# The second output projection of a hybrid decoder as seven block products instead of eight

## The chip, the core and the metric

The kernel runs on one core of a Trainium2 chip. The metric is the device time of one execution in microseconds (us), less is better. The engines that the text names: TensorE (PE, with its weight loads as PEld), VectorE (DVE), ScalarE (ACT), GpSimd (POOL) and SyncE (SP), which issues nearly all DMAs.

## The reference

One step of a two-layer decoder: a prompt of 2048 positions and a sample group of 8 x 4 positions, model width 1024, branch width 2048. Layer 0 is gated linear attention, layer 1 sliding-window attention. What the change touches is the end of layer 1: the attention output `o`, gated, times the second output weight (2048 x 1024), added to the residual stream.

```python
def swa_out(o, gate, w_out):
    bsz, seq_len = o.shape[:2]
    return (o.reshape(bsz, seq_len, BRANCH_WIDTH) * jax.nn.silu(gate)) @ w_out
...
q_p, g_p = swa_query(hp, b_norm[j], b_w_in[j], b_q_norm[j], pos_p)
hp = hp + swa_out(swa_banded(q_p, k_p, v_p, b_sinks[j]), g_p, b_w_out[j])
```

## The kernel before

**Numbers as pairs.** Every large product is fp32 in effect: each operand is held as two fp16 tiles, high and low, and a block product is three passes (`PASSES`: high x high, high x low, low x high). `split` makes such a pair: the high part on ACT, the low part on DVE or POOL. A product of a 128 x 128 block (stationary) with a 128 x 512 block (moving) is three matmuls.

**Stages.** (1) Layer 0: heads 0 to 3, each in four blocks of 512 positions (`Blk`), with the sample group beside it. (2) The first output projection, 16 chunks of 128 positions (`a_out`), with residual, norm and the transposed input of layer 1 (`uT`). (3) Attention of layer 1: 4 groups x 16 chunks = 64 blocks (`BBlk`), in a loop over n = 0..66 in which iteration n projects block n and does the scores of block n-2 and the values of block n-3. `ORDER` is a hand-written interleaving of the two attention parts with the projection steps ("f"), and while `pin` is set, TensorE keeps the order in which the program emits its matmuls. In n = 64..66 there is no block left to project, and the steps "f" are the first chunks of the last stage. (4) The second output projection.

**Last stage.** `out_steps(wo, half, ogs, finish, c)` takes one chunk c and one half of the 1024 output columns: it loads four transposed tiles of the gated output from DRAM (`ogd2`, written by `spill_og`), runs 16 contraction tiles x 3 passes = 48 matmuls into one bank of tag `pj` (two buffers), and `b_finish` adds the residual (`hd`) on DVE and stores. All 16 chunks for half 0 come first, then all 16 for half 1, so each chunk is loaded and transposed twice. `out_sample` does the same for the 32 sample positions, with the weight as the stationary operand.

**Weights ahead of time.** `GroupW` (weights of layer 1) and `wob` (the second output weight, two halves) are prepared beside the earlier stages: `Unit.prepare` loads 256 KB into `wraw` (three buffers), splits it into `pst` (two buffers), and stores the pair to DRAM from POOL's queue. These steps stand in a list `prep`, from which the blocks of layer 0 take `PR[j]` at a time and the first output projection five per chunk; `behind` gives them a lower priority. Later `steps()` fetches them as tiles `W` (12 buffers of 512 KB): eight for the next group at chunk 12 of each group, eight for half 0 at chunk 12 of the last group, eight for half 1 inside the last stage.

Outside the pinned loop a scheduler with its own model of the engines decides the order of instructions on each engine; engines then run their queues strictly in that order. A tile with a tag shares that tag's buffers; a buffer comes free when the last reader of the tile before is done.

Of the kernel before, what the change touches and what calls it, by code (L numbers as in the profile page):

```python
# [9 lines left out]
F32 = mybir.dt.float32  # L10
# [34 lines left out]
OSC = 1.0 / (SOG * SW)  # L45
OA = SQ * SST
# [8 lines left out]
PR = (1, 4, 2, 0)  # L55
# [17 lines left out]
def _body(tc, nc, cp, sb, ps, dr, i, o):  # L73
# [69 lines left out]
    ogd2 = [dr.tile([P, 2, BW], F16, tag=f"oge{c}", name=f"oge{c}") for c in range(NCH)]  # L143
# [478 lines left out]
    def sproj_steps(tiles, nk, act_hi_lo):  # L622

        box = []

        def one(x, w):
# [207 lines left out]
    wob = [out_w(i["b_w_out"][0], half, None) for half in range(2)]  # L834
    prep = [f for w in gw + wob for f in w.prepare()]
# [169 lines left out]
    def out_steps(wo, half, ogs, finish, c):  # L1005
        ot = []

        def load():
            t = T("uT", [P, 4, 8, P], F16, 4)
            for q in range(4):  # L1010
                ot.append(t[:, q])
                nc.sync.dma_start(ot[q], ogs[c][:, q % 2, q // 2 * D : q // 2 * D + D], transpose=True)

        st, box = proj_steps(lambda: PT("pj", [P, 512], bufs=2), lambda k, a: ot[k // 8 * 2 + a][:, k % 8, :], wo, 16)
        return [load] + st + [lambda: finish(half, c, box[0])]

# [34 lines left out]
    def out_sample(wo, half, finish_s):  # L1051
        st, total = sproj_steps(wo.cols(4), 16, lambda: ogTs[0])

        def fin():
            t = T("ssg", [P, 4, SMP], F32, 1)
            total(t, 0, 4, OSC)
# [21 lines left out]
    lead = 4  # L1078
    aout[0][0]()
    todo = []  # L1080
    for c in range(lead):
        todo += [aout[c + 1][0]] + aout[c][1][0] + aout[c][1][1]
    weave(prev_tail, todo)
    for c in range(lead, tail):
        aout[c + 1][0]()
        weave(aout[c][1][0] + aout[c][1][1], some(5))
        if c == 7:
            for half, w in enumerate((wo, wo1)):
                run(out_sample(w, half, a_finish_s))
# [21 lines left out]
    class BBlk:  # L1111
# [98 lines left out]
        def attend_steps(self):  # L1210
# [73 lines left out]
    class SampleB:  # L1284
# [22 lines left out]
        def steps(self):  # L1307
# [141 lines left out]
            def att_3(tq):  # L1449
# [13 lines left out]
                dve.scalar_tensor_tensor(of, pO.rearrange("p x b t -> p x (b t)"), 2.0**-20, self.sg[:, :, tk], ALU.mult, ALU.mult)  # L1463
# [17 lines left out]
    def b_finish(half, c, pp):  # L1481
        cs = slice(half * 512, half * 512 + 512)
        hr = T("E", [P, 512], F32, 2)
        nc.sync.dma_start(hr, hd[c][:, cs])
        y = T("st", [P, 512], F32, 2)
        dve.scalar_tensor_tensor(y, pp, OSC, hr, ALU.mult, ALU.add)  # L1486
        nc.sync.dma_start(o["y"][0, c * P : (c + 1) * P, cs], y)
# [12 lines left out]
    bout = [out_steps(wob[0], 0, ogd2, b_finish, c) for c in range(3)]  # L1500
    for t in range(-3, NKV * NCH):
# [11 lines left out]
        elif n < NKV * NCH + 3:  # L1513
            fill = bout[n - NKV * NCH][1:]
# [24 lines left out]
    run(out_steps(wob[0], 0, ogd2, b_finish, 3))  # L1539
# [96 lines left out]
```

## Time and profile before

| | us |
|---|---|
| median of 3 runs | 2900.65 |
| lowest, highest | 2900.28, 2902.48 |
| the profiled execution | 2899.76 |
| its span | 2898.0 |

The span runs from the first to the last instruction; 1.8 us of the profiled execution lie outside it. The stages by the span's clock: layer 0 to about 1130 us, the first output projection to about 1525, attention to about 2589, the second output projection to the end. The page gives busy times by engine, the span in 40 slices, and groups of instructions; the answers of the trace give the same for any window, and for every idle stretch of an engine what ended it.

### The profile page before, as it was taken

What the parts mean: (1) busy time and instruction counts of PE and PEld (TensorE: products, weight loads), DVE (VectorE), ACT (ScalarE), POOL (GpSimd) and SP (SyncE); (2) the same over time, 40 slices, a digit from 0 to 9 for tenths busy, and PEclk for the clock granted to TensorE, in tenths of its full rate; (3) what the DMA queues carried; (4) which work ended last, traced back from release to release, by engine and by line L of the source; (5) the groups of instructions that cost most, each with busy time, mean ns of one, the idle gap of its engine ahead of it and who ended that gap; (6) DMA issues with size and microseconds to landing.
All of it is one profiled execution on the core that took longest, in us unless ns stands there. A gap on an engine that the chain in (4) does not pass through costs nothing.

```text
span 2898.0 us, 51309 instructions
## 1 busy us (share of the span) xinstructions
PE 2769.2 (96%) x19198; PEld 1401.8 (48%) x19198; DVE 1661.5 (57%) x3543; ACT 1386.7 (48%) x3289; POOL 1012.0 (35%) x1407
## 2 busy tenths in 40 slices
PE   6899999999999999997999999999899999999999
PEld 4445444444454444444444555555555555544444
DVE  5766787687768775333214666677777767730000
ACT  6655655465556554333213555566666666620000
POOL 1241233222322221022105676566566557510000
PEclk9999999999999999998999999999999999999999
DMA  8351344124313524799866565767866777898874
GB/s 211 85 124 44 88 120 128 37 84 151 97 41 101 162 69 114 158 238 260 186 167 142 109 131 122 192 119 129 170 114 130 169 132 138 162 214 170 182 148 96
DMA packets 813331, 393.86 MB, mean 136 GB/s; under 512 B 687760, under 2 KB 740952, under 8 KB 813048
## 3 DMA queue, kind: packets, MB, share of 16 engines
q1 hardware_dynamic: 802040, 361.14, 56.3%
q0 software_dynamic: 8960, 29.37, 2.8%
q8 instruction: 150, 2.46, 0.4%
q14 instruction: 101, 0.83, 0.1%
q10 hardware_dynamic: 2080, 0.07, 0.0%
HBM read 132.61 MB, written 101.25 MB: 81 GB/s over the span
## 4 chain that ended last, share of the span: by engine, by line
PE 59%; DVE 10%; ACT 9%; DMA 9%; issue 7%; POOL 5%; SPq 1%; POOLq 0%; ACTq 0%; DVEq 0%
PE pj L99 45%; PE tr L99 6%; PE o L99 4%; PE kv L99 3%; DMA pre<-pst 2%; ACT o L1237 2%; DMA wraw<-in_a_w_in_dram 2%; DVE v L195 1%; DMA pst<-v 1%; ACT v L194 1%; PE lev L99 1%; DVE o L1232 1%; POOL pre L245 1%; DVE W L195 1%; DVE lev L1232 1%
## 5 line engine op out<-in xcount | busy, mean ns | idle before, releaser
L99 PE MATMUL pj<-W,uT 128*128 128x512 f16 x6600 | 1529.0, 381 | 6.6 <-DVE sg L475 3.4
L99 PEld LDWEIGHTS <-uT 128*128 128x128 f16 x8224 | 788.1, 98 | 892.6 <-issue 49.3
L99 PE MATMUL tr<-W,uT 128*128 128x512 f16 x1536 | 365.5, 379 | 0.0
L183 POOL TENSOR_SCALAR rs_m<-ss 128x1 f32<-128x1 f32 (+3 forms) x190 | 44.6, 235 | 757.7 <-ACT og L608 243.6
L1237 ACT ACTIVATE o<-o,mx 128x256 f32<-128x256 f32 (+1 forms) x384 | 168.6, 439 | 181.5 <-DVE mx L1232 172.1
L192 POOL TENSOR_TENSOR ogT<-og,ogT 128x512 f16<-128x512 f32 x132 | 162.1, 1228 | 168.3 <-ACT ogT L191 163.8
L99 PEld LDWEIGHTS <-X 128*128 128x128 f16 x2496 | 159.9, 98 | 120.9 <-issue 20.7
L99 PE MATMUL pj<-uT,W 128*128 128x512 f16 (+1 forms) x912 | 187.0, 356 | 27.1 <-DMA uT<-ogT 23.6
L1232 DVE CUSTOM_DVE_ANT_0 o<-o,madd,nsink 128x256 f32<-128x256 f32 (+1 forms) x384 | 184.0, 479 | 46.8 <-PE o L99 41.8
L195 DVE SCALAR_TENSOR_TENSOR v<-o,v 128x512 f16<-128x512 f32 (+1 forms) x192 | 129.0, 672 | 116.3 <-ACT v L194 98.4
L184 POOL TENSOR_TENSOR rs_r<-rs_m,mhalf 128x1 f32<-128x1 f32 (+2 forms) x186 | 185.5, 998 | 14.7
L99 PEld LDWEIGHTS <-W 128*128 128x128 f16 x2576 | 132.8, 99 | 115.0 <-issue 20.1
L1486 DVE SCALAR_TENSOR_TENSOR st<-pj,E 128x512 f32<-128x512 f32 x32 | 22.1, 692 | 269.8 <-PE pj L99 260.0
L505 POOL TENSOR_TENSOR E<-bt 128x256 f32<-128x256 f32 x96 | 74.3, 774 | 197.4 <-DVE X L192 117.7
L245 POOL DMA_DIRECT2D pre<-pst x104 | 72.3, 695 | 190.7 <-DVE pst L195 155.9
L99 PE MATMUL pj<-W,v 128*128 128x512 f16 x576 | 128.3, 379 | 0.0
L99 PE MATMUL o<-gl,X 128*128 128x256 f16 (+1 forms) x768 | 114.0, 272 | 10.2 <-DMA X<-qe 5.4
L99 PEld LDWEIGHTS <-sth 128*128 128x128 f16 x1984 | 100.3, 98 | 39.4 <-DMA sth<-v 11.2
L99 PEld LDWEIGHTS <-v 128*128 128x128 f16 x768 | 74.5, 98 | 92.6 <-issue 4.5
L646 ACT ACTIVATE ssg<-pj 128x64 f32<-128x64 f32 (+1 forms) x16 | 3.5, 240 | 236.8 <-PE pj L99 231.4
L194 ACT ACTIVATE v<-o 128x512 f16<-128x512 f32 (+1 forms) x192 | 111.3, 580 | 7.4 <-DMA sth<-v 3.7
L191 ACT ACTIVATE ogT<-og 128x512 f16<-128x512 f32 x132 | 82.2, 623 | 64.7 <-DVE og L611 44.2
(341 smaller groups left out, 4331.3 us busy)
## 6 DMA issues: line engine op xcount, KB each, us to landing
pre<-pst POOLq DMA_DIRECT2D x104, 256.0 KB, 3.8
W<-pre SPq DMA_DIRECT2D x52, 512.0 KB
ogd<-ogT SPq DMA_DIRECT2D x68, 256.0 KB
wraw<-in_a_w_in_dram SPq DMA_DIRECT2D x64, 256.0 KB
wraw<-in_b_w_in_dram SPq DMA_DIRECT2D x64, 256.0 KB
oge<-ogT SPq DMA_DIRECT2D x64, 256.0 KB
wraw<-in_a_w_out_dram SPq DMA_DIRECT2D x32, 256.0 KB
X<-in_x_prompt_dram SPq DMA_DIRECT2D x32, 256.0 KB
```

Of the source, the lines that this page charges most:

```text
L99: return order(nc.tensor.matmul(*a, **k))
L183: pool.tensor_scalar(m[:n, :k], ss, a, b, ALU.mult, ALU.add)
L184: pool.tensor_tensor(r[:n, :k], m[:n, :k], mhalf[:n, :k], ALU.pow)
L191: act(hi, src, AF.Copy)
L192: eng.tensor_tensor(lo, src, hi, ALU.subtract)
L194: act(hi, src, AF.Copy, scale=sc)
L195: dve.scalar_tensor_tensor(lo, src, sc, hi, ALU.mult, ALU.subtract)
L245: nc.gpsimd.dma_start(self.pre[:, :, half * 512 : half * 512 + 512], t)
L505: pool.tensor_tensor(Ev[:, :, 0, :], ref, btv[:, :, 0, :], ALU.subtract)
L1232: dve.tensor_tensor_reduce(pm[:, z], pm[:, z], madd.rearrange("p a b -> p (a b)")[:, (2 - nk) * P :], -0.125, nsink[:, g * GRP + h : g * G ...
L1237: act(pm[:, z], pm[:, z], AF.Exp, scale=-1.0, bias=nm_[:, h : h + 1], accum_out=bx["sum"][:, h : h + 1])
L1486: dve.scalar_tensor_tensor(y, pp, OSC, hr, ALU.mult, ALU.add)
```

## The change

The gated outputs of two chunks (c0, c1) and the two halves of the contraction form a 2 x 2 block matrix, the weight another (contraction half x column half). A Strassen scheme in Winograd's form computes the four output blocks from seven block products instead of eight. One block product is 8 contraction tiles x 3 passes = 24 matmuls.

- **Seven weight forms** (f0..f6: the blocks and sums of blocks) are made in `prep` in place of the two halves: for each of 8 contraction tiles, four raw loads of 256 KB, four subtractions on POOL, seven splits and seven stores. The raw tiles take `wraw`, `qT` and `kT`, the staging tiles `pst` and, after layer 0, also `qe`, `ke` and `Sh`. `PR` goes from 1 to 2 in its first place; the first output projection takes six steps in its first chunks and seven per chunk later.
- **Four sums of the gated outputs** per pair of chunks (`Pair.sums`) are made on chip from the transposed pairs: high + low, sums and differences on DVE, and a new split.
- `Pair.steps(n)` is product n with its finish on ACT and DVE; intermediate sums stay in SBUF (`s1`, `v`, `u2`, `u3`) or in a PSUM bank (`p5`). Each chunk is loaded and transposed once.
- All seven forms (14 MB for 8 MB) are fetched around the end of attention: three into buffers of `uT` and one into `W` in n = 56..61, three more in n = 64..66. Pair 0 fills n = 64..66, its sums being emitted at the end of n = 64.
- `spill_halves` stores the gated outputs in runs of 256 elements (before 512), split by contraction half, and their fp32 tile moves from `og` (one buffer) to `wraw` (three).
- The sample group uses f0 and f3 for one half, and f0, f2 and f5 for the other (24 contraction tiles instead of 16).

```diff
-PR = (1, 4, 2, 0)
+PR = (2, 4, 2, 0)
...
+    def form_steps(m):
+        b, f = {}, {}
+        def load():
+            for n, (r, z) in enumerate(((0, 0), (0, 1), (1, 0), (1, 1))):
+                t = T(("wraw", "wraw", "qT", "kT")[n], [P, 512], F32, 3 if n < 2 else 1)
+                k = UP[m] + 2 * r
+                nc.sync.dma_start(t, i["b_w_out"][0][k * P : (k + 1) * P, z * 512 : z * 512 + 512])
+                b[r, z] = t
+            f[0], f[3], f[5] = b[0, 0], b[1, 0], b[1, 1]
+        def put(n):
...
+            if n == 2:
+                sub(b[0, 1], b[0, 0])
+            elif n == 1:
+                sub(b[1, 1], f[2])
+            elif n == 4:
+                sub(b[1, 1], b[0, 1])
+            elif n == 6:
+                sub(b[1, 0], f[1])
+            t = T(tags[0], [P, 2, 512], F16, 2)
+            tags.append(tags.pop(0))
+            split((t[:, 0], t[:, 1]), f[n], SWB)
+            nc.gpsimd.dma_start(wfd[n][:, m], t)
+        return behind([load] + [lambda n=n: put(n) for n in (0, 2, 1, 3, 6, 5, 4)], 200)
...
+    tags += ["qe", "ke", "Sh"]
...
-                og = T("og", [P, 512], F32, 1)
+                og = T("wraw", [P, 512], F32, 3)
...
+    PRODS = (("pj", 0), ("pj", 3), ("o", 2), ("tr", 1), ("tr", 4), ("o", 5), ("pj", 6))
+    RAW = ("v", "sg") * 4 + ("sth", "pst") * 2
+    FORM = ("X", "ogT", "X", "ogT", "qe", "ke", "qe", "ke")
+    TEMP = ("wraw", "Sh", "wraw", "Sh", "wraw", "bt", "bt", "og")
...
+        def load(self, x):
+            first = (("og", "lvm"), ("qT", "kT"), ("bt", "bt"), ("S", "sg"))[x]
+            ts = [T(tag, [P, 8, P], F16, BUFS.get(tag, 2)) if self.p == 0 else ring("raw", RAW, [P, 8, P], F16) for tag in first]
+            for hl in range(2):
+                nc.sync.dma_start(ts[hl], ogd2[2 * self.p + x // 2][:, hl, x % 2], transpose=True)
...
+            def one(z):
+                whole(3, z)
+                whole(2, z)
+                dve.tensor_tensor(a[3, z], a[3, z], a[2, z], ALU.add)
+                put(2, z, a[3, z])
+            def two(z):
+                whole(0, z)
+                dve.tensor_tensor(a[2, z], a[0, z], a[2, z], ALU.subtract)
+                dve.tensor_tensor(a[0, z], a[3, z], a[0, z], ALU.subtract)
+                put(3, z, a[0, z])
+            def three(z):
+                put(4, z, a[2, z])
+            def four(z):
+                whole(1, z)
+                dve.tensor_tensor(a[1, z], a[1, z], a[0, z], ALU.subtract)
+                put(5, z, a[1, z])
...
+                    mm(box[0], self.l[n][a][:, k, :], wf[w](k, b), start=x == 0, stop=x == 23)
...
+        if n in (TOT - 8, TOT - 5, TOT - 3):
+            wform_big((0, 2, 1)[(TOT - 8, TOT - 5, TOT - 3).index(n)], 4)
+        if n == TOT - 4:
+            wform(3)
+        if n == TOT - 2:
+            pairs[0].load(0)
+        if n == TOT - 1:
+            for x in (1, 3, 2):
+                pairs[0].load(x)
+        if n == TOT:
+            wform_big(4, 4)
+            run(pairs[0].sums())
+        if n == TOT + 1:
+            wform(5)
+            pairs[1].load(0)
+            pairs[1].load(1)
+        if n == TOT + 2:
+            wform(6)
+            pairs[1].load(3)
+            pairs[1].load(2)
...
-    run(out_sample(wo, 0, b_finish_s))
-    for c in range(NCH):
-        run(out_steps(wo1, 1, ogd2, b_finish, c))
-        if c == 8:
-            run(out_sample(wo1, 1, b_finish_s))
+    for p_ in range(NCH // 2):
+        more = []
+        if p_ + 1 < NCH // 2:
+            nxt = pairs[p_ + 1]
+            if p_ > 0:
+                more += [lambda x=x, nxt=nxt: nxt.load(x) for x in (0, 1, 3, 2)]
+            more += nxt.sums()
+        weave([f for n in range(0 if p_ else 6, 7) for f in pairs[p_].steps(n)], more)
```

Here `whole(x, z)` adds the high and low tile of block x (half z of its positions and tiles) into fp32, and `put(n, z, t)` splits a sum into the pair that product n reads.

More of the change, by code (lines that the diff above doesn't have):

```diff
@@ L142, in _body @@
     ogd = [dr.tile([P, 2, BW], F16, tag=f"ogd{c}", name=f"ogd{c}") for c in range(NCH)]
-    ogd2 = [dr.tile([P, 2, BW], F16, tag=f"oge{c}", name=f"oge{c}") for c in range(NCH)]
+    ogd2 = [dr.tile([P, 2, 2, D], F16, tag=f"oge{c}", name=f"oge{c}") for c in range(NCH)]
+    wfd = [dr.tile([P, 8, 2, 512], F16, tag=f"wf{n}", name=f"wf{n}") for n in range(7)]
     ud = [dr.tile([P, 2, D], F16, tag=f"ud{c}", name=f"ud{c}") for c in range(NCH - 4, NCH)]
@@ L620, in spill_og, with spill_halves, sproj_steps @@
         nc.sync.dma_start(dst[:, :, h * 512 : (h + 1) * 512], ot)
-    def sproj_steps(tiles, nk, act_hi_lo):
+    def spill_halves(og, c, g):
+        ot = T("ogT", [P, 2, 512], F16, 2)
+        split((ot[:, 0], ot[:, 1]), og, eng=pool)
+        nc.sync.dma_start(ogd2[c].rearrange("p a k x -> p (a k) x")[:, :, g * 256 : (g + 1) * 256], ot.rearrange("p a (k x) -> p (a k) x", k=2))
+    def sproj_steps(tiles, nk, act_hi_lo, kts=None):
         box = []
+        kts = kts or list(range(nk))
         def one(x, w):
@@ L1002, in _body @@
         cur = nxt
[L1005 to L1015, printed above, removed]
     def a_out(c):
@@ L1049, in a_out, with out_sample @@
         return load, out
-    def out_sample(wo, half, finish_s):
-        st, total = sproj_steps(wo.cols(4), 16, lambda: ogTs[0])
+    def out_sample(tiles, half, finish_s, kts=None, sc=OSC):
+        st, total = sproj_steps(tiles, len(kts or range(16)), lambda: ogTs[0], kts)
         def fin():
             t = T("ssg", [P, 4, SMP], F32, 1)
-            total(t, 0, 4, OSC)
+            total(t, 0, 4, sc)
             pt = PT("tr", [SMP, 512], bufs=2)
@@ L1078, in _body @@
     lead = 4
+    few = 2
+    each = (len(prep) - 3 * few) // (tail - lead + 1) + 1
     aout[0][0]()
@@ L1081, in _body @@
     for c in range(lead):
[L1082 removed]
+        todo += [aout[c + 1][0]] + mix(aout[c][1][0] + aout[c][1][1], some(few if c else 0))
     weave(prev_tail, todo)
+    tags += ["qe", "ke", "Sh"]
     for c in range(lead, tail):
         aout[c + 1][0]()
[L1086 removed]
+        weave(aout[c][1][0] + aout[c][1][1], some(each))
         if c == 7:
             for half, w in enumerate((wo, wo1)):
[L1089 removed]
+                run(out_sample(w.cols(4), half, a_finish_s))
     def rope_mul(eng, t1, t2, src, ct, st):
@@ L1480, in _body, with wform_big @@
     ORDER = "AffffffffBfAfffffffAfffAfBffff"
[L1481 to L1487, printed above, removed]
+    PRODS = (("pj", 0), ("pj", 3), ("o", 2), ("tr", 1), ("tr", 4), ("o", 5), ("pj", 6))
+    wf = {}
+    def wform_big(n, parts=1):
+        t = T("uT", [P, 8, 2, 512], F16, 4)
+        for x in range(parts):
+            ks = slice(x * 8 // parts, (x + 1) * 8 // parts)
+            nc.sync.dma_start(t[:, ks], wfd[n][:, ks])
+        wf[n] = lambda k, hl, s=ALL: t[:, k, hl, s]
@@ L1499, in _body @@
     boundary = []
-    bout = [out_steps(wob[0], 0, ogd2, b_finish, c) for c in range(3)]
+    pairs = [Pair(p_) for p_ in range(NCH // 2)]
+    TOT = NKV * NCH
     for t in range(-3, NKV * NCH):
@@ L1513, in _body @@
         elif n < NKV * NCH + 3:
-            fill = bout[n - NKV * NCH][1:]
+            x = 2 * (n - TOT)
+            fill = pairs[0].steps(x) + pairs[0].steps(x + 1)
         lists = {
```

109 lines of the change are left out of this document (93 added, 16 removed).

## Prediction

> **What bounds the kernel now.** First the page's busy times and its 40 slices.
>
> ```profile
> span 2898.0 us, 51309 instructions
> PE 2769.2 (96%) x19198; PEld 1401.8 (48%) x19198; DVE 1661.5 (57%) x3543; ACT 1386.7 (48%) x3289; POOL 1012.0 (35%) x1407
> PE   6899999999999999997999999999899999999999
> DVE  5766787687768775333214666677777767730000
> DMA  8351344124313524799866565767866777898874
> ```
>
> TensorE is busy nearly everywhere, VectorE is empty in the last four slices, and the DMA queues are fullest in slices 17 to 20 and 33 to 36. The busy time by windows shows what these mean: the first output projection with its weight preparation (three rows), attention, its end, and the last stage.
>
> ```profile
> 1130.00:1240.00 110.00, 110.00 (x508) 47.19 (x506) 44.50 (x90) 41.68 (x80) 10.10 (x19) 1.00 0.72 161
> 1280.00:1365.00 85.00, 64.34 (x508) 33.28 (x507) 28.93 (x46) 26.22 (x48) 22.56 (x35) 0.90 0.96 256
> 1365.00:1525.00 160.00, 160.00 (x745) 72.73 (x744) 31.50 (x52) 29.99 (x62) 14.25 (x28) 1.00 0.76 183
> 1525.00:2480.00 955.00, 925.61 (x7892) 515.95 (x7891) 638.49 (x1647) 561.83 (x1676) 613.87 (x804) 0.99 0.68 138
> 2480.00:2589.00 109.00, 102.03 (x916) 56.70 (x913) 66.05 (x172) 56.92 (x170) 46.12 (x62) 1.00 0.99 193
> 2589.00:2898.00 309.00, 305.22 (x1644) 142.41 (x1641) 22.45 (x35) 0.81 (x3) 0.00 (x0) 1.00 0.75 153
> ```
>
> Columns: length, then busy time of PE, PEld, DVE, ACT, POOL, granted clock, DMA share, GB/s. The last stage has no gap on PE until its final 3.8 us, at full clock; DVE works 22 us of 309 and POOL not at all. So its length is its matmuls, and a matmul less is its whole time less. The other two places that matter are 1280 to 1365, where PE loses 85 - 64.34 = 20.7 us, and 2480 to 2589, where it loses 7.0 us at a DMA share of 0.99.
>
> **Step 1, the removed products.** The timeline of DVE in the last stage shows one finish per chunk and half, and the group of its matmuls their number.
>
> ```profile
> 2842.46 0.69 DVE L1486 SCALAR_TENSOR_TENSOR st<-pj,E 128x512 f32<-128x512 f32 x1 [9.67 <-PE pj L99]
> 2852.82 0.69 DVE L1486 SCALAR_TENSOR_TENSOR st<-pj,E 128x512 f32<-128x512 f32 x1 [9.67 <-PE pj L99]
> L99 PE MATMUL pj<-W,uT 128*128 128x512 f16 x1377 | 298.0, 379 | 0.0
> ```
>
> Two finishes stand 10.36 us apart, for 48 matmuls: 0.2158 us each (the mean of 379 ns contains overlap). Before: 16 chunks x 2 halves x 48 = 1536. After: 8 pairs x 7 products x 24 = 1344. Removed: 192 x 0.2158 = **41.4 us**. Of this, nothing falls in n = 64..66, which hold 48 steps each before and after; the tail behind them goes from 29 x 48 = 1392 to 50 x 24 = 1200 matmuls.
>
> [...]
>
> **Step 2, the sample group.** The second half takes 24 contraction tiles instead of 16, 64 matmuls more.
>
> ```profile
> 2720.46 3.65 PE L99 MATMUL pj<-ogTs,W 128*128 128x64 f16 x128
> 2723.95 4.91 PE L99 MATMUL pj<-W,uT 128*128 128x512 f16 x22
> ```
>
> 128 took 3.49 us to the next group's start, so 64 add **+1.7 us**.
>
> **Step 3, the sums in the last stage.** Per pair, DVE does 8 additions of high and low, 8 sums, 8 low parts and 11 finishing operations, 35 in all; ACT 9. The nearest groups of 128x512:
>
> ```profile
> L488 DVE TENSOR_TENSOR E<-qT,kT 128x512 f32<-128x512 f32 x16 | 11.4, 714 | 28.4 <-ACT kT L427 28.3
> L192 DVE TENSOR_TENSOR X<-E,X 128x512 f16<-128x512 f32 x128 | 96.2, 752 | 14.2 <-ACT X L191 13.8
> L192 DVE TENSOR_TENSOR qe<-kT,qe 128x512 f16<-128x512 f32 x64 | 66.3, 1037 | 25.0 <-ACT qe L191 24.6
> L191 ACT ACTIVATE ogT<-og 128x512 f16<-128x512 f32 x132 | 82.2, 623 | 64.7 <-DVE og L611 44.2
> ```
>
> At 0.72 us, 35 operations are 25 us against 7 x 24 x 0.2158 = 36.3 us of matmuls; ACT has 9 x 0.62 = 5.6 us. The same subtraction of a split takes 752 ns in one stage and 1037 in attention, where POOL is busy; at 1037 it would be 36.3 us, still even, and in the last stage POOL has 0.00. So the matmuls hide the sums, **0 us**, from pair 1 on: they stand one pair ahead. Transposed loads fall from 4 per 10.36 us to 8 per 36.3 us, so DMA (0.75 there) and SP get lighter; the eight weight fetches inside the stage go. The last matmul is followed by one DVE operation and one store, as before.
>
> **Step 4, the hand-over from attention, n = 56..66.** This is where I expect to lose. Moved here: fetches of 14 MB for 4 MB. Windows around one earlier fetch of 4 MB (2060 to 2090), the one of now (2540 to 2560), the end, and eight such fetches in the quiet end of the first projection:
>
> ```profile
> 2060.00:2070.00 10.00, 8.75 (x109) 4.89 (x107) 8.34 (x22) 6.27 (x19) 7.69 (x9) 1.00 1.14 272
> 2070.00:2080.00 10.00, 7.54 (x60) 4.18 (x60) 5.45 (x15) 3.83 (x11) 2.41 (x3) 1.00 0.95 215
> 2080.00:2090.00 10.00, 7.70 (x85) 4.40 (x86) 6.45 (x19) 6.38 (x18) 5.83 (x8) 1.00 0.92 188
> 2540.00:2550.00 10.00, 9.00 (x68) 4.67 (x65) 5.80 (x15) 4.85 (x14) 1.24 (x3) 1.00 1.14 218
> 2550.00:2560.00 10.00, 7.47 (x69) 3.89 (x69) 5.71 (x20) 5.59 (x18) 2.56 (x4) 1.00 1.16 199
> 2570.00:2580.00 10.00, 7.05 (x54) 3.39 (x52) 1.01 (x3) 1.42 (x6) 3.01 (x5) 1.00 1.07 196
> 1498.00:1510.00 12.00, 12.00 (x57) 5.49 (x56) 0.69 (x1) 0.63 (x2) 0.00 (x0) 1.00 0.88 337
> ```
>
> PE loses 1.25 + 2.46 + 2.30 = 6.0 us around the earlier 4 MB, and 1.00 + 2.53 = 3.5 us around the present one: the fetches stand in SP's queue ahead of the transposes of the probabilities, and `values`, whose place in PE's order is pinned, waits; all behind it on PE waits too. So 0.88 to 1.5 us per MB. I charge the 6 MB of f4, f5 and f6, which meet 16 transposed loads at a share above 1, at 0.88: +5.3; the other 4 MB more, spread over six iterations, at half a microsecond: +2.0. Then buffers: `X` holds the queries of block 63 until its scores are done, and product 3 of pair 0 stands ahead of those in PE's order, so its `X` can only be the one that product 2 gives back; an ACT and a DVE operation (0.62 + 0.75) lie bare, and likewise one for product 5, whose `ke` is held by the sample group: +2.6. Together **+10 us**. Ends: -3 (three buffers for `og` in place of one may spare waits) and +25 (the row of 337 GB/s gives 12 us for 4 MB, so 10 MB bare are 30 us, less what product 0 to 4 can cover).
>
> The `oge` stores go to 512-byte runs, 64 stores over attention; its DMA share of 0.68 leaves room: 0 us, and at most 2 if their packets cost twice.
>
> **Step 5, the weight preparation beside the first output projection.** Its groups, waits, and the longest stall:
>
> ```profile
> L245 POOL DMA_DIRECT2D pre<-pst x49 | 34.0, 693 | 117.2 <-DVE pst L195 93.3 <-DVE ss L305 6.5 <-issue 6.1
> L194 ACT ACTIVATE pst<-wraw 128x512 f16<-128x512 f32 x32 | 20.1, 627 | 62.3 <-DMA pre<-pst 47.5 <-issue 10.3 <-DMA wraw<-in_b_w_out_dram 2.9
> ACT pst L194 <- DMA pre<-pst: 63.5, 25, 6.4
> PE pj L99 <- DVE st L1031: 18.1, 3, 12.9
> 1355.35 0.80 PE L99 MATMUL pj<-ogTs,uT 128*128 128x64 f16 x16 [12.92 <-DVE st L1031]
> 1350.00:1360.00 10.00, 4.42 (x107) 4.29 (x106) 4.33 (x8) 4.21 (x9) 3.35 (x5) 0.50 0.97 228
> L1141 POOL TENSOR_TENSOR kT<-kT,S 128x512 f32<-128x512 f32 x64 | 81.3, 1270 | 0.2
> ```
>
> Now 49 steps run here. A step's ACT part waits for a staging buffer, that is for a store to land; its DVE part waits behind; and the residual addition of the projection (L1031), further back in DVE's queue, comes late, so PE has no free bank: 18.1 of the 20.7 us. After: 72 steps, of which 6 lie before 1240, where PE has no gap and DVE 60% free: 0 us, 6 x 0.75 = 4.5 if that cover is gone. The rest: 64 splits for 49 (15 more of ACT 0.63, DVE 0.69, POOL issue 0.69) and 32 subtractions of 1.27 us = 41 us on POOL, behind which the norm's small POOL operations queue; bytes 26 MB for 24.5 MB at a share near 1. Staging grows from 2 to 8 buffers, so the wait for stores should go; in its place come the raw tiles in `qT` and `kT`, one buffer each, whose load stands on SP until the last subtraction of the tile before, with everything behind it on SP (the projection's own residual loads among them). I see no reason for one to be larger: **0 us**, from -18 (the stall goes) to +15 (8 rounds x 4.5 us for a bare load, 36 us, for the 20.7).
>
> **Step 6, layer 0.** `PR` moves 9 steps into the blocks j = 0: 9 x 0.75 = 6.8 us of DVE, which is about 70% busy there in the slices. **+2 us**, 0 to 7.
>
> **Sum**, against the profiled execution of 2899.76: -41.4 + 1.7 + 0 + 10 + 0 + 2 = -27.7, so 2872.1. The median lies 0.9 higher: 2900.65 - 27.7 = **2873 us**.
>
> **Rivals.**
> - *The preparation gets smooth:* step 5 at -18. For it: the wait is one for two staging buffers, and there are eight. Against: the queues are also full. 2873 - 18 = 2855.
> - *The hand-over starves:* step 4 at +25. For it: share above 1 already. Against: PE lost only 7.0 us there so far. 2873 + 15 = 2888.
> - *Slower, the preparation paces PE:* each of the 8 rounds leaves DVE's and POOL's queues waiting for a raw load, with L1031 behind. Two banks of 10.36 us are the slack; at 8.5 us a round (7 of load, 1.5 of reduced clock) it is 68 us for the 20.7, and 2873 + 47 = 2920. It decides from (20.7 + 27.7 + 5.8)/8 = 6.8 us a round. Against: 4 MB came in 12 us above, and a round loads 1 MB.
>
>   The clock price in it is seen: after the wait of 12.92 us the granted clock is 0.50 over 10 us. [...]
> - *Nothing saved:* the products are there but PE waits for sums or loads in every pair, 36.3 us becoming 41.4. Against: step 3. About 2900 to 2915.
> - *The change does not do what it says:* the matmul count would not fall by 128. Negligible.
>
> **Chances.** Forecast, 2862 to 2884: 0.50. Smooth preparation, below 2862: 0.20. Starved hand-over, 2884 to 2895: 0.16. Within 0.2% (5.8 us, about what a measurement of this kernel can tell from none), partly by the fourth rival: 0.07. Slower: 0.07. Range 2849 to 2895: it takes the centres of the second and third case in, and leaves out some 0.05 below and 0.14 above.
>
> **What would show it.** About 19070 matmuls. In the tail, finishes 5.18 us apart and no gap on PE: step 1 right; PE waiting there for `X`, `ogT`, `qe` or `ke`: step 3 wrong. Windows of the hand-over: PE idle of 7 now, 17 expected. The window around 1280 to 1365: idle of 20.7, unchanged; if it falls below 5, the second rival; past 50, the third. What would make it wrong most: a scheduler that orders attention anew because of `og` and the later fetches.

## The result, and the profile after

| | before | after |
|---|---|---|
| median of 20 runs | 2900.57 | 2906.89 |
| lowest, highest | 2892.86, 2906.78 | 2898.57, 2916.24 |
| profiled execution, its span | 2899.76, 2898.0 | 2902.2, 2900.4 |

The ratio of after to before is **1.0024**, with a 95% interval of 1.0014 to 1.0034: slower by a little more than the measurement can tell. The forecast was 2873 us, and its range ended at 2895. All times by stage below are from the profiled executions, which differ by +2.4 us; a profile says where time went, the ratios say how much.

The page of after: the busy times, and the 40 slices of PE, DVE, granted clock and DMA share.

```profile
span 2900.4 us, 51645 instructions
PE 2740.0 (94%) x19070; PEld 1385.9 (48%) x19070; DVE 1854.8 (64%) x3815; ACT 1440.1 (50%) x3385; POOL 1059.9 (37%) x1463
PE   6899999999999999997999999999999999978999
DVE  5766787677768775346213665677767767756553
PEclk9999999999999999998999999999999999989999
DMA  8351334124312533799765565867867788887542
```

PE is busy 29.2 us less than before (2769.2), as seven products for eight should make it, and yet the span has not shrunk: slice 36 (2538 to 2610 us) has a 7 and slice 37 an 8 where before had 9, and the granted clock dips beside them (0.88 and 0.93 over these two slices). To find where the loss builds up, take events that both kernels have and compare their times. On DVE's timeline these are the gated output of a chunk in layer 0, the last finish of the first output projection, and the gated outputs of attention's blocks 60 and 63; before first, then after.

```profile
1061.35 0.74 DVE L611 SCALAR_TENSOR_TENSOR og<-o,rs_r,sg 128x512 f32<-128x512 f32 x1
1528.20 0.69 DVE L1031 SCALAR_TENSOR_TENSOR st<-pj,X 128x512 f32<-128x512 f32 x1 [5.54 <-PE pj L99]
2535.66 0.69 DVE L1279 SCALAR_TENSOR_TENSOR og<-kv,sg 128x512 f32<-128x512 f32 x1
2583.27 0.69 DVE L1279 SCALAR_TENSOR_TENSOR og<-kv,sg 128x512 f32<-128x512 f32 x1 [12.26 <-PE kv L99]
```

```profile
1073.57 0.74 DVE L614 SCALAR_TENSOR_TENSOR og<-o,rs_r,sg 128x512 f32<-128x512 f32 x1
1540.33 0.69 DVE L1064 SCALAR_TENSOR_TENSOR st<-pj,X 128x512 f32<-128x512 f32 x1 [5.54 <-PE pj L101]
2542.34 0.69 DVE L1315 SCALAR_TENSOR_TENSOR wraw<-kv,sg 128x512 f32<-128x512 f32 x1
2616.84 0.69 DVE L1315 SCALAR_TENSOR_TENSOR wraw<-kv,sg 128x512 f32<-128x512 f32 x1 [1.40 <-PE kv L101]
```

After stands behind by 12.2 us late in layer 0, by 12.1 at the end of the first projection, by 6.7 at block 60, by 33.6 at block 63, and by 2.4 at the end. So layer 0 lost 12.2, the first projection nothing, attention regained 5.4, three iterations (the hand-over) lost 26.9, and the rest won 31.2. One correction: product 6 of pair 0, planned for the tail, was drawn forward by the scheduler into the hand-over (it starts at 2571.33 us); its 24 x 0.2158 = 5.2 us of work belong to the tail. With that, the hand-over lost **21.7** and the tail won **26.0** of the 39.7 hoped for. These are single executions. In the 19 profiled kernels that can be set side by side, the `og` of layer 0 shown above comes at 1068.4 to 1073.9 us in the five with `PR` at 2, and at 1055.3 to 1065.4 in the fourteen with it at 1, so one such offset can be some 5 us off.

What PE waited for in after from 2530 to 2660 us (total, times, longest):

```profile
PE o L101 <- ACT X L194: 6.4, 1, 6.4
PE pj L101 <- DMA kT<-oge: 5.7, 1, 5.7
PE o L101 <- DVE v L198: 3.4, 1, 3.4
PE pj L101 <- DMA qT<-oge: 3.0, 1, 3.0
PE o L101 <- DVE ogT L195: 2.9, 2, 2.2
```

Product 1 of pair 0 waits for its transposed pair in `qT` and `kT`, product 2 for its sum (`ogT`), the next scores for DVE (`v`), and, behind attention, product 2 of pair 1 for its own (`X`, 6.4). SP's queue in after shows why the loads are late (start, time in the queue):

```profile
2534.87 0.58 SPq L1532 DMA_DIRECT2D W<-wf  x1
...
2538.92 0.79 SPq L1532 DMA_DIRECT2D W<-wf  x2
2539.80 4.44 SPq L1279 DMA_TRANSPOSE sth<-v  x1
2544.34 4.01 SPq L1279 DMA_TRANSPOSE pst<-v  x1
2548.44 1.01 SPq L1532 DMA_DIRECT2D W<-wf  x2
2549.54 0.38 SPq L1525 DMA_DIRECT2D uT<-wf  x1
2550.02 1.94 SPq L1556 DMA_TRANSPOSE qT<-oge  x1
...
2558.74 1.29 SPq L1556 DMA_TRANSPOSE kT<-oge  x1
...
2562.90 1.59 SPq L1556 DMA_TRANSPOSE bt<-oge  x1
```

The fetches of f5 and f6, written for iterations 65 and 66, go out as soon as their `W` buffers come free, ahead of pair 0's loads. `qT` and `kT` themselves come free only when block 63's queries are normed, rotated and split, and by then product 0 is running: product 1, 24 matmuls later, needs both, and `kT` is issued 8.7 us after `qT`, behind two more transposes of probabilities and the queries of block 63. On DVE, the same lateness shows a second time:

```profile
2567.94 0.69 DVE L1569 TENSOR_TENSOR Sh<-bt,bt 128x512 f32<-128x512 f16 x1 [11.56 <-DMA bt<-oge]
2568.55 0.49 DVE L1268 CUSTOM_DVE_ANT_0 lev<-lev,madd,nsink 128x256 f32<-128x256 f32 x1
```

An addition of pair 0's sums (L1569) stood at the head of DVE's queue for 11.56 us, waiting for `bt`, and the softmax of block 62 (L1268) started 0.61 us after the addition, behind it. PE's scores for it began at 2565.61, themselves late by the wait for `kT`, so here this second lateness cost 2 us and no more. That DVE kept to its order shows in these 2 us: the scores were done at about 2566.5 (2565.61 + 0.91).

### The profile page after: what moved, and what is told of

It reads as the page before. It is cut to its first block, busy times and chain, and to the rows that moved or that the text cites. A ratio compares the mean times of both kernels' runs of the same rounds, so it can differ in the third digit from the quotient of the medians.

```text
span 2900.4 us, 51645 instructions
## 1 busy us (share of the span) xinstructions
PE 2740.0 (94%) x19070; PEld 1385.9 (48%) x19070; DVE 1854.8 (64%) x3815; ACT 1440.1 (50%) x3385; POOL 1059.9 (37%) x1463
## 4 chain that ended last, share of the span: by engine, by line
PE 38%; DVE 8%; DMA 7%; ACT 6%; issue 4%; POOL 4%; SPq 1%; DVEq 0%; POOLq 0%; ACTq 0%
PE pj L101 24%; PE tr L101 8%; PE o L101 4%; ACT o L1273 2%; PE kv L101 2%; ACT v L197 1%; DVE v L198 1%; DVE o L1268 1%; DMA pst<-v 1%; DMA sg<-oge 1%; DMA sth<-v 1%; DVE lev L1268 1%; DMA X<-qe 1%; DMA kT<-in_b_w_out_dram 1%; ACT lev L1273 1%
## 5 line engine op out<-in xcount | busy, mean ns | idle before, releaser
L101 PE MATMUL pj<-W,uT 128*128 128x512 f16 x5064 | 1193.2, 381 | 8.4 <-DVE sg L478 2.6
L101 PEld LDWEIGHTS <-uT 128*128 128x128 f16 x6880 | 643.0, 98 | 713.9 <-issue 44.5
L101 PEld LDWEIGHTS <-X 128*128 128x128 f16 x2752 | 185.2, 98 | 169.6 <-issue 30.2
L101 PE MATMUL pj<-uT,W 128*128 128x512 f16 (+1 forms) x912 | 188.3, 357 | 26.9 <-DMA uT<-ogT 24.2
L1268 DVE CUSTOM_DVE_ANT_0 o<-o,madd,nsink 128x256 f32<-128x256 f32 (+1 forms) x384 | 184.1, 479 | 42.0 <-PE o L101 37.0
L101 PE MATMUL pj<-W,v 128*128 128x512 f16 x736 | 177.6, 382 | 3.8 <-DVE E L1064 3.8
L101 PEld LDWEIGHTS <-v 128*128 128x128 f16 x1008 | 98.5, 99 | 130.1 <-issue 16.4
L101 PE MATMUL pj<-W,sg 128*128 128x512 f16 x592 | 146.6, 381 | 1.2 <-DVE E L1064 1.2
L195 POOL TENSOR_TENSOR ogT<-og,ogT 128x512 f16<-128x512 f32 x68 | 88.2, 1297 | 158.0 <-ACT ogT L194 153.5
L101 PEld LDWEIGHTS <-sg 128*128 128x128 f16 x800 | 78.2, 98 | 97.9 <-issue 6.8
L1273 ACT ACTIVATE lev<-lev,mx 128x256 f32<-128x256 f32 (+1 forms) x128 | 56.5, 442 | 121.2 <-DVE mx L1268 119.1
L101 PE MATMUL kv<-rmask,sth 128*128 128x64 f16 x1984 | 104.7, 193 | 7.3 <-DMA sth<-v 7.3
```

The source lines that it names most:

```text
L101: return order(nc.tensor.matmul(*a, **k))
L195: eng.tensor_tensor(lo, src, hi, ALU.subtract)
L1268: dve.tensor_tensor_reduce(pm[:, z], pm[:, z], madd.rearrange("p a b -> p (a b)")[:, (2 - nk) * P :], -0.125, nsink[:, g * GRP + h : g * G ...
L1273: act(pm[:, z], pm[:, z], AF.Exp, scale=-1.0, bias=nm_[:, h : h + 1], accum_out=bx["sum"][:, h : h + 1])
```

## The experiments

All ratios are to the kernel before, run beside it on the same chip. "Hand-over" is the time from the `og` of block 60 to that of block 63, "rest" from there to the end; product 6 of pair 0 lies in the first in some kernels and in the second in others, so their sum is what compares.

| kernel | ratio (95% interval) | hand-over | rest | sum |
|---|---|---|---|---|
| before | 1 | 47.6 | 314.7 | 362.3 |
| after | 1.0024 (1.0014 to 1.0034) | 74.5 | 283.6 | 358.1 |
| e1_pr | 0.9983 (0.9972 to 0.9995) | 75.5 | 283.6 | 359.1 |
| e2_nosums | 1.0013 (1.0002 to 1.0024) | 68.2 | 286.6 | 354.8 |
| e3_nofetch | 0.9985 (0.9970 to 0.9999) | | | |
| e4_late | 1.0059 (1.0036 to 1.0081) | 63.9 | 305.0 | 368.8 |
| e5_early | 1.0003 (0.9990 to 1.0017) | 72.9 | 279.2 | 352.0 |
| e6_pin | 1.0005 (0.9991 to 1.0019) | 68.4 | 286.5 | 354.9 |
| e7_all | 0.9953 (0.9935 to 0.9971) | 56.0 | 292.8 | 348.7 |
| e8_early_pin | 0.9958 (0.9941 to 0.9975) | 60.4 | 286.4 | 346.8 |
| e9_halves | 0.9960 (0.9945 to 0.9975) | 57.0 | 294.0 | 350.9 |
| e10_halves_f | 0.9952 (0.9934 to 0.9969) | 61.9 | 286.6 | 348.5 |
| e11_pool | 0.9956 (0.9940 to 0.9971) | 55.1 | 296.8 | 351.9 |
| e12_nosums | 0.9970 (0.9955 to 0.9985) | 56.9 | 295.4 | 352.4 |
| e13_neither | 0.9893 (0.9876 to 0.9909) | 42.5 | 290.8 | 333.3 |
| e14_nofetch | 0.9937 (0.9922 to 0.9952) | 56.8 | 286.5 | 343.3 |
| e15_six | 0.9972 (0.9960 to 0.9985) | 66.9 | 287.7 | 354.7 |
| e16_six_ord | 0.9972 (0.9957 to 0.9987) | 62.4 | 291.8 | 354.1 |
| e17_keep | 0.9942 (0.9919 to 0.9964) | 56.9 | 288.4 | 345.3 |
| e18_keep_f | 0.9961 (0.9945 to 0.9977) | 65.2 | 285.2 | 350.4 |

### Layer 0

```diff
-PR = (2, 4, 2, 0)
+PR = (1, 4, 2, 0)
```

> Only PR goes back to 1 in the blocks j = 0; everything else is as in the kernel after, so that 9 steps of the weight preparation go back from layer 0 to the first output projection. Where the time went by the traces: after stands 12.2 us behind before when layer 0 ends, and it was put at 2. Theory A (the nine steps cost that, as DVE and ACT work ahead of layer 0's own): the offset at the end of layer 0 falls to 2 or less, the first output projection gives 0 to 5 of it back, and the median falls by 7 to 12, from 2906.9 to 2895 to 2900. Rival B (the offset is that of another order of layer 0's instructions and not of the steps): it stays at 8 or more, and the median within 4 us of 2906.9.

The ratio fell by 0.0041, 12 us, and the offset at the end of layer 0 was gone. The nine steps went back to the first projection and cost next to nothing there: its last finish stood at 1527.57 us, before's at 1528.20. Theory A holds. What PE waits for at the state update (`kv`) from 300 to 1180 us, first before, then after, then e1_pr:

```profile
PE kv L99 <- ACT v L194: 5.9, 5, 1.9
```

```profile
PE kv L101 <- ACT v L197: 9.7, 4, 3.2
```

```profile
PE kv L101 <- ACT v L197: 3.4, 3, 1.7
```

The loss comes in three steps of 3 to 5 us, one in each of heads 1 to 3 (the offset is 5.1, 9.1 and 12.2 us after them), three more preparation steps each. That is 12.2 / 9 = 1.36 us a step, about a split's ACT part and DVE part one after the other (0.63 and 0.69). The `kv` wait accounts for only 3.8 us of the 12.2 against before, and 6.3 against e1_pr.

### The hand-over, one part at a time

> Pair 0 makes no sums: its products 2 to 5 take the transposes of the first half block as they are (left out: 24 operations on DVE and 8 on ACT for the first two chunks, whose y comes out otherwise). All fetches and all transposed loads stay. The hand-over, from the og of block 60 to that of block 63, lost 27 us against before. Theory A (the sums stand in DVE's queue ahead of the softmax of blocks 62 and 63, and wait there for a late load): the loss falls to 8 to 14, median 2889 to 2895. Rival B (the bytes: 14 MB of weight forms at a DMA share above 1): it stays at 22 or more, median 2902 to 2908. Theory C (the late loads in SP's queue, for which product 1 waits 8.7 us on PE itself): it falls to 15 to 20, since PE's own waits for qT and kT stay.

The cut gained 3 us, which is B's range, and the waits for `kT` (5.9) and `qT` (4.9) stayed. By the table the hand-over's loss fell from 26.9 to 20.6, just above C's range, and the rest grew by 3.0. Theory A falls as the sole cause.

> The forms f4, f5 and f6 are not fetched (left out: 6 of the 14 MB; products with them take f0, f2 and f3 in their place, so y comes out otherwise). Sums and transposed loads stay. Rival B (the bytes) and theory C (their place in SP's queue ahead of pair 0's transposed loads) both say that the hand-over's 27 us falls to 8 to 15 and the waits for qT and kT go (5.7 and 3.0 us): median 2892 to 2897. Theory A (the sums in DVE's queue, whatever is fetched): 20 or more stay, median above 2900. It is read beside the next one, which keeps the bytes.

It gained 11 us. The table has no stretches for it, so just the ratio is read.

```diff
-            wform_big(4, 4)
+            wform_big(4, 4, later)    # program order on SP
...
-            wform(5)
+            wform(5, later)
...
-            wform(6)
+            wform(6, later)
```

> The same three fetches, all 6 MB, but held in program order on SP: f4 behind iteration 64, f5 behind 65, f6 behind 66, so that pair 0's transposed loads and the transposes of the probabilities stand ahead of them. Theory C (the place in the queue): the waits for qT and kT shrink to 2 us or less together and the hand-over gains two thirds or more of what the kernel without the fetches gains, 8 to 13 us, median 2894 to 2899. Rival B (the bytes): it gains less than a third of that, and product 4 or 5 waits for f4 or f5 in place of the loads, median 2902 to 2908.

Against both: 10 us slower than after. The waits for the loads did shrink (`kT` 2.6, `qT` 1.0), and the hand-over was 5.4 us shorter (63.9 against 74.5 less the 5.2 of product 6, which here stands behind it), but the forms then came late:

```profile
2603.26 1.04 PE L101 MATMUL o<-W,qe 128*128 128x512 f16 x2 [4.75 <-DMA W<-wf]
2628.21 1.01 PE L101 MATMUL pj<-W,S 128*128 128x512 f16 x2 [15.80 <-DMA W<-wf]
```

So the place in the queue matters, in both directions: 6 MB ahead of the loads make the loads late, and behind them the forms.

### Two edits that mend, and both together

e5_early moves the queries of block 63 to `wraw`, of which attention needs one buffer, so that `qT` and `kT` are free an iteration sooner; e6_pin keeps product 6 where the program has it.

```diff
-                qn = T("qT", [P, 512], F32, 1)
+                end = g * NCH + c == NKV * NCH - 1
+                qn = T(*(("wraw", [P, 512], F32, 3) if end else ("qT", [P, 512], F32, 1)))
...
-        if n == TOT - 2:
+        if n == TOT - 8:
             pairs[0].load(0)
+        if n == TOT - 2:
+            pairs[0].load(1)
```

> One edit to after: block 63's normed and rotated queries go to two buffers of wraw, so that qT and kT are free one iteration sooner and pair 0's second transposed pair (and its first, into og and lvm) is loaded before iteration 63. Sums, fetches and PR stay. Theory C (the late loads): product 1's waits for qT and kT (3.0 and 5.7 us in after) go, and with them the slowed clock behind them; the ratio to before falls from 1.0024 to 0.9980 to 1.0000, some 7 to 12 us. Rival B (the bytes of the fetches, whoever waits): the waits move to the transposes of the probabilities or to S and bt, and the ratio stays above 1.0010.

> One edit to after: the pin of PE's order is held through product 6 of pair 0, which in after was drawn forward to 2576 us, into the middle of the last iterations, so that nothing was left to stand between pair 0 and pair 1's first sums. Theory D (the tail's loss of 8.5 us is the 6.4 us wait of pair 1's product 2 for its sums plus the slowed clock, for want of 24 matmuls that product 6 would have been): that wait falls to 1.5 us or less and the tail gains 5 to 9 us. But the 5.2 us of product 6 also filled a gap of the hand-over, which grows by up to 5.2 us: ratio between 1.0005 and 1.0024. Rival (product 6 where it stood cost nothing and saved a gap of its own length): ratio 1.0024 to 1.0045.

> Together: PR back to 1 in the blocks j = 0, block 63's buffers (early loads of pair 0), the pin through product 6, and the fetches in order: f4 and f5 behind iteration 64, f6 behind 65. Should the parts add up: 12 us from PR (measured), 7 to 10 from the early loads, 4 to 6 from the order of product 6 and the fetches: ratio 0.9920 to 0.9950, about 2875 to 2883 us on this chip. If the bytes of the fetches bind (rival B), f5 or f6 comes late and PE waits for W or uT by 5 us or more: ratio 0.9965 or above.

> As the one before without the order of the fetches: f4, f5 and f6 stand on SP as early as their buffers allow, as in after. If their early place is what makes the transposes of the probabilities late (4.4 and 4.0 us at 2540 to 2548 in after), this is 3 to 6 us slower than the one before; if a late fetch costs more than an early one, as when all three were put back, it is 3 us or more faster.

e5_early: the waits for `qT` and `kT` are gone. The gain by the ratios is 6 us, somewhat less than C's range; part of it came back at once as other waits:

```profile
2562.33 0.23 PE L101 MATMUL kv<-rmask,sth 128*128 128x64 f16 x2 [2.96 <-DMA sth<-v]
2580.53 1.01 PE L101 MATMUL pj<-W,S 128*128 128x512 f16 x2 [4.85 <-DMA W<-wf]
```

e6_pin gained 5.5 us by the ratios: no wait for `X` is longer than 1.3 us where one was 6.4, as theory D has it; the rest gained 2.3 in the profiles (286.5 against 283.6 with product 6's 5.2 added), less than D's 5 to 9. Together with `PR` they came to 0.9953 and 0.9958, 21 and 19 us below after: **faster than both kernels**, by 14 and 12 us against before, and 3 to 4 short of the sum of the three parts (23.5). The order of the fetches made no difference that can be measured. In e7_all, where product 6 stands in its place too, PE waits 7.9 us for `X` in the rest, so that place alone does not remove the wait.

### What holds PE then

In e7_all PE waits for DVE: for the softmax of the sample group, which stands behind an addition that waits for `bt`. First PE's wait, then DVE's.

```profile
2548.97 1.01 PE L101 MATMUL o<-gl,X 128*128 128x256 f16 x4 [6.39 <-DVE mxs L1463]
```

```profile
2540.78 0.69 DVE L1570 TENSOR_TENSOR Sh<-bt,bt 128x512 f32<-128x512 f16 x1 [4.50 <-DMA bt<-oge]
```

The next three shift or lighten that work: the sums in two halves behind the sample's step, on two orders of the fetches, and half the additions on POOL.

```diff
+        if boundary:
+            boundary.pop(0)()
...
-            run(pairs[0].sums())
+            late = pairs[0].sums()
+            run(late[:4])
...
         if n == TOT + 1:
+            run(late[4:])
```

> From e7_all (ratio 0.9953), one edit: the sums of pair 0 are emitted in two halves, those of products 2 and 3 behind iteration 64 and those of 4 and 5 behind 65, and the sample's step of each iteration ahead of them. In e7_all the loads are early, and what PE waits for is now DVE: 6.4 us for the sample's softmax and 2.6 us for block 62's, while DVE is busy 9.15 and 10.00 us of two stretches of 10 with the 24 operations. Theory A in its second place (with the loads early, the order of the sums in DVE's queue is the next wait): those waits fall below 3 us together and the hand-over gains 5 to 9 us with the clock, ratio 0.9920 to 0.9940. Rival B (bytes: whatever is put in order, 6 MB and the transposes take their time): the wait moves to sth, pst or W, and the ratio stays at 0.9945 or above.

> From e8_early_pin (ratio 0.9958) the same edit: halves, and the sample's step first. Here the fetches of f5 and f6 stand early, at the release of the buffers. The tail of e8_early_pin was 286.4 us from the last og, that of e7_all 292.8, where pair 1's loads stood behind f6; so this should keep the shorter tail and gain the same 5 to 9 us in the hand-over if theory A holds: ratio 0.9915 to 0.9940. If the transposes of the probabilities behind the early fetches bind (4.3 us for one in e8_early_pin), it stays at 0.9950 or above.

> From e9_halves, one more edit: the second half of the additions of high and low goes to POOL, in every pair (4 of 24 sums of a pair; POOL did 1.27 us for a 128x512 operation in attention and is empty behind it). If DVE's time is what product 2 to 5 wait for, 4 x 0.69 us less on DVE gains 1 to 3 us in the hand-over and in pair 1, and nothing from pair 2 on: ratio 0.0005 to 0.0010 below that of e9_halves. If the chain of one sum is what counts, POOL's 1.27 for 0.69 makes it 1 to 3 us slower.

None moved the ratio. In e9_halves the wait for `mxs` is 6.39 as it was, since the scheduler put the same addition ahead of the softmax again. The ratios of e9_halves and e10_halves_f lie in their rivals' ranges, but the longest wait of the hand-over stayed the one for `mxs` (5.3 in e10_halves_f), so the rivals are not shown by it. Does the time hang on the sums at all?

> From e8_early_pin: pair 0 makes no sums, its products 2 to 5 take the first transposes as they are (left out: 24 operations of DVE and 8 of ACT; the first two chunks of y come out otherwise). With the loads late, in e2_nosums, the same cut gained 3 us (1.0024 to 1.0013). Theory A in its second place: with the loads early the sums are the bound, and the cut gains 8 to 13 us, ratio 0.9915 to 0.9930. Rival B (bytes): it gains 4 us or less, ratio 0.9945 or above.

Leaving them out made it no faster (0.9970 against 0.9958, intervals that overlap): as the sole cause theory A falls in its second place as well. But the wait had changed its name; SP's queue in e12_nosums, and PE:

```profile
2557.74 1.95 SPq L1526 DMA_DIRECT2D uT<-wf  x4
2559.79 2.40 SPq L1533 DMA_DIRECT2D W<-wf  x3
2562.30 4.85 SPq L1280 DMA_TRANSPOSE sth<-v  x1
```

```profile
2572.14 0.29 PE L101 MATMUL kv<-rmask,sth 128*128 128x64 f16 x2 [8.05 <-DMA sth<-v]
```

With no sums in the way, seven fetches of 512 KB stand in a row ahead of the transpose of the probabilities, and PE waits 8.05 us for that. No run left the sums out with the fetches put in order, so whether their bytes or their place does it is open. Two runs complete the table.

> From e8_early_pin: neither the sums of pair 0 nor the fetches of f4, f5 and f6 (left out: 24 operations of DVE, 8 of ACT and 6 MB; y comes out otherwise). With e8_early_pin, e12_nosums and e14_nofetch it makes a table of two by two. From the og of block 60 to that of 63 before took 47.6 us, after 74.5, e8_early_pin 60.4, e12_nosums 56.9. Theory E (either of the two holds PE by itself, so that taking one away uncovers the other): here the stretch is at 50 or less, and the ratio at 0.9900 to 0.9925. Theory F (something else holds it: 8 transposed loads of pair 0 beside the transposes of the probabilities): 54 or more, ratio 0.9935 or above.

> From e8_early_pin: the fetches of f4, f5 and f6 left out (6 MB; products with them take f0, f2 and f3, y comes out otherwise), the sums kept. Theory E: the sums alone still hold PE, by the late bt at the head of DVE's queue, and the stretch from the og of block 60 to that of 63 stays at 54 to 60. Rival B (it was the bytes): 50 or less, as without both, and the ratio at 0.9900 to 0.9925.

| ratio, and sum of the two stretches | fetches of f4 to f6 | without |
|---|---|---|
| sums of pair 0 | 0.9958, 346.8 | 0.9937, 343.3 |
| without | 0.9970, 352.4 | **0.9893**, 333.3 |

Theory E holds: by the ratios one cut alone gives -6 us (no fetches) or +3 (no sums), neither clear of the noise, and both together give -19, well clear of it. The hand-over alone, with the same products in it in all four, shows it best: 60.4 us with both, 56.8 without the fetches, 56.9 without the sums, 42.5 without either. In e8_early_pin PE is busy 47.1 of the 60.4 us at a mean granted clock of 0.86, in e13_neither 40.3 of 42.5 at 1.00; so of the 17.9 us between them 11.1 are waits and 6.8 longer busy time at the lower clock. Each of the two holds PE by itself and hides the other. In the rest, both kernels without pair 0's sums lose again, at pair 1's first sum: PE waits 7.8 us (e12_nosums) and 7.6 (e13_neither) for `X`, where e8_early_pin has 0.4. That takes back what e12_nosums, 3.5 us shorter in the hand-over, had won. What makes that sum late was not taken apart.

Windows of e13_neither, in which PE loses 2.2 us of 30:

```profile
2540.00:2550.00 10.00, 9.04 (x79) 5.03 (x77) 7.49 (x23) 6.00 (x18) 1.54 (x4) 1.00 1.06 184
2550.00:2560.00 10.00, 9.95 (x71) 5.29 (x71) 4.61 (x17) 4.16 (x13) 1.02 (x2) 1.00 0.54 113
2560.00:2570.00 10.00, 8.83 (x86) 5.05 (x85) 4.17 (x11) 4.49 (x16) 4.05 (x7) 1.00 0.89 153
```

Last, how the sums hold it: a product without sums put in front (e15, e16), or the additions pinned behind the softmaxes on DVE (e17, e18).

```diff
-            fill = pairs[0].steps(x) + pairs[0].steps(x + 1)
+            fill = [f for z in (0, 1, 6, 2, 3, 4)[x : x + 2] for f in pairs[0].steps(z)]
```

> From e10_halves_f (0.9952): product 6 of pair 0, which needs no sum, comes third, and its bank is held until product 4 has made u3; products 2, 3, 4 move back by 24 matmuls (5.2 us) each and product 5 stands behind attention; f6 is fetched ahead of f4 and f5. If the first sum is late by the waits seen (5.4 us for the sample's softmax behind it, 2.3 for ogT, and a clock of 0.62 to 0.67), 5.2 us of raw matmuls in front cover most: 4 to 8 us, ratio 0.9925 to 0.9940. If DVE's queue is held by the late bt whatever PE does, the sample's softmax stays late and so does PE: within 2 us of 0.9952.

> The same order of products on e9_halves (0.9960), with the fetches held in order: f6 and f4 behind iteration 64, f5 behind 66. The loads of pair 0 stand ahead of every one of these fetches, and f5 is not needed before the tail. If bytes ahead of the transposes are what is left, this is the best of all, 0.9915 to 0.9935; if f6 comes late, which product 6 now needs one iteration sooner, PE waits for W by 5 us or more and it is at 0.9955 or above.

```diff
-                dve.tensor_tensor(t, hi, lo, ALU.add)
+                x_ = dve.tensor_tensor(t, hi, lo, ALU.add)
+                if self.p == 0:
+                    tc.keep_in_program_order(x_)
```

> From e9_halves (0.9960), one edit: the additions of high and low of pair 0 are held in program order on DVE, so that the softmax of block 62 and the sample's stand ahead of them and not behind. The table of two by two said: without the fetches the sums cost 12.7 us (0.9937 against 0.9893), and in every kernel with sums PE waited 4.8 to 6.4 us for the sample's softmax, which stood behind an addition that waited 2.4 to 4.5 us for bt. If that one place in DVE's queue is the cost, the wait for mxs falls under 2 us and some 6 of it comes back, ratio 0.9930 to 0.9945. If the sums are late in any order, product 2 waits for X and ogT in its place, by 4 us or more: 0.9955 or above.

> The same on e10_halves_f (0.9952), where f5 and f6 are fetched early. Same two readings: 0.9920 to 0.9940 if the place in DVE's queue is the cost; 0.9948 or above if product 2 waits for X and ogT by 4 us or more, or for sth behind the fetches, in its place.

Product 6 in front did not make it faster (0.9972 both, outside both forecasts for e15_six; the intervals overlap with those of the kernels that they start from): f6 is then needed an iteration sooner (4.70 us for `W` in e16), the sample's softmax is about as late as before (4.8 and 6.2 us), and in e16 PE waits 11.2 us for an `X` in the rest. The pin on DVE did what it was meant to, and nothing was won that the intervals can tell (0.9942 and 0.9961). The first lies in the range of the first reading, the second in that of the second. The waits are those of the second reading in both: 8.2 us for `X` in e18_keep_f, and in e17_keep:

```profile
2552.34 0.60 PE L101 MATMUL o<-gl,X 128*128 128x256 f16 x4 [0.77 <-DVE mxs L1463]
2558.16 1.03 PE L101 MATMUL o<-uT,X 128*128 128x512 f16 x2 [5.22 <-ACT X L194]
```

The sample's softmax is in time (0.77 for 6.39), and now product 2 waits 5.22 us for its sum. So with these loads the sums are late in either order: their inputs come into buffers that block 63 gives back, and only two products stand in front of the first use. A version with the pin on DVE and product 6 in front was not run.

## Why the prediction was wrong, step by step

| | predicted | measured |
|---|---|---|
| steps 1 to 3, the last stage | -39.7 | -26.0 |
| step 4, the hand-over | +10 | +21.7 |
| attention ahead of it (an end of step 4) | 0 | -5.4 |
| step 5, first projection | 0 | -0.1 |
| step 6, layer 0 | +2 | +12.2 |
| sum, profiled executions | -27.7 | +2.4 |

The sum missed by 30.1 us: 13.7 in the last stage, 11.7 in the hand-over and 10.2 in layer 0, less the 5.4 of attention. (From the last finish of the first projection to the `og` of block 60, before took 1007.5 us, and the 18 other profiled kernels of the table 999.0 to 1004.5; whether the three buffers for `og` do it was not tested.)

**Step 1 was right.** PE has 19070 matmuls, as forecast. In the tail of after, away from its start, they run as before; the first row, and the row behind the last, of a stretch in which 25 matmuls start:

```profile
2779.67 0.38 PE L101 MATMUL pj<-W,sg 128*128 128x512 f16 x1
2785.07 0.59 PE L101 MATMUL pj<-uT,sth 128*128 128x512 f16 x2
```

That is 5.40 / 25 = 0.216 us each, the worth that the prediction gave a matmul. Windows of before's and after's last stage, and of an inner stretch of after:

```profile
2583.30:2898.00 314.70, 310.92 (x1712) 145.31 (x1710) 23.81 (x37) 1.44 (x4) 1.16 (x1) 1.00 0.76 152
```

```profile
2616.80:2900.40 283.60, 265.57 (x1536) 124.51 (x1534) 156.44 (x253) 38.25 (x67) 1.16 (x1) 0.97 0.49 109
2760.00:2890.00 130.00, 130.00 (x773) 61.96 (x772) 63.85 (x103) 16.09 (x28) 0.00 (x0) 1.00 0.39 90
```

PE idles 18.0 us where before idled 3.8, and 14.1 of it are waits at pair 1's first sum (7.1) and for the finish of a product (7.0). From 2760 to 2890 it idles not at all, with DVE half busy: there **step 3 held**, the sums lie beside the matmuls.

**Step 3 failed for pair 1, and step 2 by a wait it did not name.** "They stand one pair ahead" is true only if the pair ahead has something left to cover with. Pair 1's loads wait for attention's own buffers (`v` and `sg`), and with product 6 gone forward only two raw products (10.4 us) stood before its first sum: 6.4 us of wait, at most 1.3 with product 6 in place (e6_pin), but 7.6 to 8.9 in e7_all, e9_halves, e11_pool, e12_nosums and e13_neither, where it is in place as well. So which of the two makes that sum late is in part open. Behind the first sample group PE waits 5.67 us for the finish of a product, `PE pj <- DVE st`; step 2 counted matmuls only. The trace shows what the finishes themselves waited for, the residual's load into `E`, of whose two buffers one also holds the sum `v` until product 5 is finished:

```profile
2738.17 0.69 DVE L1609 TENSOR_TENSOR E<-E,E 128x512 f32<-128x512 f32 x1 [3.50 <-DMA E<-hd]
2741.69 0.69 DVE L1609 TENSOR_TENSOR E<-E,kT 128x512 f32<-128x512 f32 x1 [1.62 <-DMA E<-hd]
```

The finish behind the second row ends when PE starts again (2743.2). No run took that wait apart.

**Step 4 is the step that failed first.** It priced the fetches by stalls per MB and named two late buffers, `X` and `ke`. The buffers that decided were others in the same diff: `qT`, `kT`, `S` and `bt`, which block 63 releases just when pair 0 is to start. Between that release and the first use stand 24 matmuls for product 1 and 48 for product 2, and through them had to go the transposed loads, with fetches in the same SP queue, and then eight operations on DVE among the softmaxes. The size lay inside the ends that the prediction kept (21.7 for 10, the end 25); that the parts do not add lay outside: bytes, late loads and sums each hold PE, and taking one away from after returns 3 to 11 us.

**Step 5 was right**, and more so than argued: with 81 steps there (e1_pr; 72 in after) it still takes about before's time, 468.4 us from the `og` of layer 0 to its last finish for 466.9. **Step 6 was mis-sized**, +2 for +12.2: it priced a step at 0.75 us of DVE, mostly hidden, and a step cost 1.36 us, about the whole length of its ACT and DVE part. The longer wait of `kv` for ACT points that way but is under half of it; that it is this chain was not tested by itself. That the nine steps cost the 12 us is shown by e1_pr.

**The rivals.** The starved hand-over came about in size, at +21.7 for its +25, though not by bytes alone, and does not explain the result alone. Neither a smooth preparation nor one that paces PE came, since the first projection is unchanged. "Nothing saved" named 2900 to 2915 us, where the time fell, but not its cause: from 2760 to 2890 us PE waits for no sum and no load. The change does what it says.

## What to carry to other kernels

When work is moved into the last iterations of a pipelined loop, list the buffers that it takes with the instruction that releases each, and price the chain from that release to its first use, through every in-order queue on the way; a price per byte misses it. When removing one suspect gains little, remove two at once before acquitting it: here two cuts of -6 and +3 us made -19 together. And a small preparation step put beside a recurrence can cost far more than its share of an engine: here 1.36 us for the 0.2 forecast.

## What was not expected of the hardware

The longer waits were paid twice, by the slower clock behind them. In after, PE's rows behind the 5.67 us wait:

```profile
2743.22 1.01 PE L101 MATMUL pj<-uT,v 128*128 128x512 f16 x2 [5.67 <-DVE st L1601]
...
2747.01 0.65 PE L101 MATMUL pj<-uT,v 128*128 128x512 f16 x2
```

Two matmuls take 1.01 us at first and 0.65 after 3.8 us. Nine start in these 3.79 us, one every 0.42 us where 0.216 is the pace elsewhere, so the wait costs nearly 2 us more. The granted clock was 0.50 over these 3.79 us and 0.99 over the 6 us behind them (2747 to 2753). A shorter wait had it too: product 1 in after took 1.03 us for two behind 3.02 us, at a granted clock of 0.50, where other waits stand close by. Not every wait of that size did: four matmuls of 256 columns took 0.61 us behind 3.24 us (at 2445.21; the clock was 1.00 to 2450), but 1.04 behind 3.51 (at 1857.02; 0.50 over the 2 us from there). Behind 3.37 us (at 2588.96) the four took 0.60, and the clock was 1.00 until 2590.1 and then 0.50 to 2596, with a wait of 1.31 us in between.
